# Grouping and order of the row transfers of an RMSNorm-matmul kernel: 40 tiles of input loaded at the outset, the first eight output tiles stored as one transfer, then loads and stores of eight tiles in turn

## The chip, the cores and the metric

The kernel runs on one core of one Trainium2 chip. The core has TensorE (PE, matrix products and transposes, written to PSUM), VectorE (DVE), ScalarE (ACT), GpSimd (POOL) and SyncE (SP), which here only issues transfers. Transfers between HBM and the on-chip memory run on the core's 16 DMA engines. The metric is the device time of one execution in microseconds (us); the number given for a kernel is the median of its timed runs. The times of the kernel before are 209.05, 209.08 and 209.09 us, so the median is 209.08.

## The reference

```python
batch, seq, dim, out_dim = 16, 1024, 512, 768
rms = np.sqrt(np.mean(x ** 2, axis=-1, keepdims=True) + eps)
x_norm = x / rms * gamma
return np.matmul(x_norm, weight).astype(np.float32)
```

`x` is 16384 rows of 512 float32 (33.55 MB), `weight` is 512 x 768 (1.57 MB), the output 16384 rows of 768 float32 (50.33 MB).

## The kernel before

The 16384 rows are cut into 128 *tiles* of 128 rows, one row to a partition. A tile of x is 262,144 bytes (2 KB to a partition), a tile of the output 393,216 bytes (3 KB to a partition). Two tiles make a *pair* `j`, and the main loop runs over the pairs 1 to 63 (pair 0 is written out ahead of it).

A tile passes these stages. SP loads it into `xt`, which has 2 buffers of 16 tiles, that is 32 tile places; tile `i` and tile `i + 32` share a place (`x_of`). POOL casts it to bf16 (`cast`, L187, into `xb`; four tiles of every 16 go by `cast_quad`, L259, into `xq`). ACT sums its squares (`square`, L195); a place of `xt` is free for the next load when both the cast and the squares of its tile are done. PE transposes the bf16 tile as 32-bit words (L229) and DVE copies the result out of PSUM (L238), or, for the tiles of `xq`, DVE transposes blocks (L270). PE multiplies with the weights (`matmuls`, L299). ACT for even tiles (L278) and DVE for odd ones (L280) scale the product by the row's reciprocal root and write it to `ot`, which has 3 buffers of 8 tiles; tile `i` and tile `i + 24` share a place. SP stores a finished group of tiles from there (`store`, L292).

All transfers but the small one of gamma are issued by SP, one after the other, in the order in which the program text makes them: the class `Order` records every operation, puts each on its engine's list in that order, and adds the waits on semaphores that reads and writes of the same cells need. If a transfer on SP has to wait, everything behind it on SP waits too.

What the change touches is the size of the transfers and their order.

- `stretches` (called for `x_first, x_size` and `o_first, o_size`) tells how tiles are grouped into transfers. Before, x is loaded as 2, 2, 4 and 8 tiles, then 8 and 8, then 16 three times (tiles 32 to 79), then 8 each. The output is stored as 1, 1, 2 and 4 tiles, then 8 each, and at the end as 4, 4, 4, 2 and 2.
- `rows` tells which rows of HBM a transfer has. A block of `t` tiles is laid so that each partition holds `t` consecutive rows; a transfer of `n` of them moves, for each partition, one piece of `n` rows. Before, `t` is the size of the load for the first 16 tiles, 16 for the next 16, and 32 from there on. So a load of 16 tiles moves pieces of 32 KB, one of 8 tiles pieces of 16 KB, a store of 8 tiles pieces of 24 KB, and the store of one tile pieces of 3 KB.
- `load_until` issues the loads up to a tile. Ahead of the loop it is called for 32 tiles (with the two weight transfers between the first and the second load). In the loop, the call at the head of a pair's turn decides when SP is given further loads; `AHEAD` is 20.

The order of transfers on SP before is therefore: the loads of tiles 0 to 31; the stores of tiles 0, 1, 2 to 3, 4 to 7; the load of 32 to 47; the stores of 8 to 15 and 16 to 23; the load of 48 to 63; the stores of 24 to 31 and 32 to 39; the load of 64 to 79; and so on, two stores and then 16 tiles of loads; after the last load (112 to 127) come the stores of tiles 88 to 127.

Of the kernel before, what the change touches and what calls it, by code (L numbers as in the profile page):

```python
# [100 lines left out]
def kernel(  # L101
# [20 lines left out]
    NT = N // P  # L122
    NP = NT // 2
    XG, OG = 16, 8
    AHEAD = 20

    def stretches(group, parts):
        first, size, i = {}, {}, 0
        for g in range(NT // group):
            for n in parts.get(g, [group]):  # L130
                for t in range(i, i + n):
                    first[t], size[t] = i, n
                i += n
        return first, size

    last = NT // OG - 1
    x_first, x_size = stretches(XG, {0: [2, 2, 4, 8], **{g: [8, 8] for g in (1, 5, 6, 7)}})
    o_first, o_size = stretches(OG, {0: [1, 1, 2, 4], last - 1: [4, 4], last: [4, 2, 2]})

    def rows(ap, i, n):  # L140
        base, t = (x_first[i], x_size[i]) if i < XG else (i - i % XG, XG) if i < 2 * XG else (i - i % (2 * XG), 2 * XG)
        return ap[base * P:(base + t) * P, :].rearrange("(p t) d -> p t d", t=t)[:, i - base:i - base + n, :]

    def sb(name, shape, dtype):
# [29 lines left out]
    def load(i):  # L174
        dst, to = x_of(i, x_size[i])
        order.transfer(SP, lambda: SP.dma_start(out=dst, in_=rows(x, i, x_size[i])), writes=to)  # L176
# [3 lines left out]
    def load_until(i):  # L180
        while starts and starts[0] < i:
            load(starts.pop(0))

    def cast(i, n=1):
        src, of = x_of(i, n)
        s = i // 8 % 2
        run(POOL, lambda: POOL.tensor_copy(out=xb[s][:, i % 8:i % 8 + n, :], in_=src), of, cells("xb", s, i % 8, n))  # L187
# [17 lines left out]
    def norms(i, n):  # L205
        for t in range(n):
            square(i + t)
        root(i, n)
# [6 lines left out]
    def norms_of_group(j):  # L215
        square(2 * j)
        square(2 * j + 1)
        if j in norm_end:
            root(*norm_end[j])
# [33 lines left out]
    def quad_of(j):  # L253
        return j // 2 if (2 * j) % XG >= XG - 4 and 2 * j >= XG else None

    def cast_quad(q):
        src, of = x_of(4 * q, 4)
        s = 4 * q // XG % 2
        run(POOL, lambda: POOL.tensor_copy(out=xq[s], in_=src), of, [("xq", s)])  # L259
        for t in range(4):  # L260
            xT_of[4 * q + t] = (xTq[s][:, t], ("xTq", s))
        words = xq[s].rearrange("p t d -> p (t d)").bitcast(F32).rearrange("p (a w) -> p a w", w=P)
        turned = xTq[s].rearrange("p t h m c -> p (t h m c)").bitcast(F32).rearrange("p (a m) -> p a m", m=P)
        for tokens in range(0, P, B):
            for features in range(0, P, B):
                quad_moves.append((turned[features:features + B, :, tokens:tokens + B],
                                   words[tokens:tokens + B, :, features:features + B], s))
# [4 lines left out]
    def move_quad(n):  # L272
        for _ in range(min(n, len(quad_moves))):
            move(*quad_moves.pop(0))
# [9 lines left out]
    def accumulator():  # L284
        return next(turns) % 3

    def store(i):
        first, n = o_first[i], o_size[i]
        s = first // OG % 3
        if i == first + n - 1:  # L290
            src = ot[s][:, first % OG:first % OG + n, :]
            order.transfer(SP, lambda: SP.dma_start(out=rows(out, first, n), in_=src), reads=cells("ot", s, first % OG, n))  # L292
# [12 lines left out]
    def matmuls(i, a, ks, feed=None):  # L305
        block, cell = xT_of[i]
        for k in ks:
            lhsT = block[:, k // 2, :, k % 2]
            hold(lhsT, cell)
            for half, lo, hi in ((0, 0, WIDE), (1, WIDE, O)):  # L310
                product(ops[a][:, lo:hi], lhsT, w_bf[:, k, lo:hi], k == 0, k == K - 1,
                        [cell, ("w", k, half)], [("ops", a, half)])
            if feed:
                feed()

    def finish_tile(i, a, engine):
        s = i // OG % 3

        before = [("ot", s, i % OG - 1)] if i == o_first[i] + o_size[i] - 1 else []
        scale(engine, ot[s][:, i % OG, :], ops[a][:, :O], rstd[:, i:i + 1],  # L320
              [("ops", a, 0), ("ops", a, 1), ("rstd", i)] + before, [("ot", s, i % OG)])
        store(i)

    def feeder(pairs, gaps, alone=False):
        queue = [(j, t, h) for j in pairs for t in range(2) for h in range(2)]
        calls = iter(gaps)

        def feed():
            for _ in range(next(calls)):
                j, t, h = queue.pop(0)  # L330
                transpose_word(j, t, h)
                if alone and h == 1:
                    evac(j, t, 1)
                elif (t, h) == (1, 1):
                    evac(j)
        return feed
# [65 lines left out]
    mid, one, two, both = ([0, 0, 1, 1, 0, 1, 1, 0], [1, 1, 0, 1, 1, 0, 0, 0], [1, 0, 1, 0, 1, 0, 1, 0],  # L402
                           [1, 1, 1, 1, 1, 1, 1, 1])
    for j in range(1, NP):
        load_until((2 * j + AHEAD + XG - 1) // XG * XG)
        if j in (1, 2):
            cast(4 * j + 4, 4)
        elif j % 8 == 4 and j + 4 < NP:
            cast(2 * j + 8, 8)
        elif j % 8 == 6 and j + 2 < NP:  # L410
            cast(2 * j + 12, 4)
        if (2 * j + 2) % XG == 0 and 2 * j + 2 < NT:
            cast_quad((2 * j + 2 + XG - 4) // 4)
        elif 2 * j >= XG:
            move_quad(3)
        if j < 4:
            norms(2 * j + 2, 2)
        for pair in norm_turns.get(j, []):
            norms_of_group(pair)
        if j < 3:  # L420
            feed = feeder([j + 1], mid if j == 1 else one, alone=j == 1)
        elif j == 3:
            feed = feeder([4, 5], both)
        elif j + 2 < NP and quad_of(j + 2) is None:
            feed = feeder([j + 2], two)
        else:
            feed = None
        for i, engine in ((2 * j, ACT), (2 * j + 1, DVE)):
            a = accumulator()
            matmuls(i, a, range(K), feed)  # L430
            finish_tile(i, a, engine)
# [48 lines left out]
```

## Time and profile before

| what | value |
|---|---|
| median of the timed runs | 209.08 us |
| the profiled execution: its time, its span | 208.56 us, 206.8 us |
| instructions in the span | 2761 |
| ACT busy, DVE busy, POOL busy | 144.5, 149.3, 59.9 us |
| HBM read, written | 35.13 MB, 50.33 MB |
| TensorE clock granted, mean | 0.992 |
| loads of 2048 KB, issue to landing | median 21.0 us (9 of them) |
| loads of 4096 KB, issue to landing | median 22.7 us (3) |
| stores of 3072 KB, issue to landing | median 16.5 us (13) |

The span is the stretch that the profile shows; the execution's time holds 1.8 us more around it. Busy times are sums over the span. "Issue to landing" is the time from SP's issuing instruction to the semaphore that tells that all of a transfer has landed; it holds the time that the transfer spends behind earlier ones. A transfer's issue is short (0.33 us for a store): SP is free again long before the data has moved.

### The profile page before, as it was taken

Reading aid. Unit: us, or ns where it says so; the run is one execution under the profiler, and the core shown is the slowest. Engines: PE = TensorE matmul, PEld = TensorE weight load, DVE = VectorE, ACT = ScalarE, POOL = GpSimd, SP = SyncE. Lnnn points to the kernel's source line nnn. Section 1 sums busy time; section 2 is a strip of 40 time slices with the busy share of each in tenths; the row PEclk is TensorE's granted clock in tenths of the full one; section 3 lists DMA queues with packets and bytes.
Section 4 is the critical chain, followed back from the end, with each engine's and each line's share of the span. In section 5 each row is a group of like instructions: output and inputs, shape, how many; then the busy total and the mean of one; then the engine's idle time right before and its main releaser. Section 6 shows DMA issues by size and latency. Waiting matters only on the chain.

```text
span 206.8 us, 2761 instructions
## 1 busy us (share of the span) xinstructions
PE 192.9 (93%) x1212; PEld 72.5 (35%) x717; DVE 149.3 (72%) x255; ACT 144.5 (70%) x343; POOL 59.9 (29%) x34
## 2 busy tenths in 40 slices
PE   7789999999999999998999999999999999999930
PEld 1234443432343333342333333433343333343300
DVE  0455647998589966998469984999569984999520
ACT  4798897868768496864977687677867787673310
POOL 2247651009300291004900660006700274000000
PEclk9999999999999999999999999999999999999996
DMA  6999999999999999999999999999999999999993
GB/s 225 423 445 428 387 385 444 456 396 428 428 445 425 417 426 455 425 409 433 431 415 436 428 445 403 439 417 447 418 441 414 437 433 441 418 442 409 414 415 141
DMA packets 5632, 85.62 MB, mean 414 GB/s; under 512 B 626, under 2 KB 628, under 8 KB 1780
## 3 DMA queue, kind: packets, MB, share of 16 engines
q1 hardware_dynamic: 5616, 85.46, 97.6%
q8 instruction: 7, 0.11, 0.2%
q14 instruction: 5, 0.04, 0.0%
q10 hardware_dynamic: 4, 0.00, 0.0%
HBM read 35.13 MB, written 50.33 MB: 413 GB/s over the span
## 4 chain that ended last, share of the span: by engine, by line
PE 71%; DMA 16%; DVE 5%; issue 2%; SPq 1%; ACT 1%; POOL 1%; ACTq 0%
PE ps L299 62%; DMA xt<-in_x_dram 16%; PE ps L229 8%; DVE ot L280 2%; DVE xTq L270 2%; DVE xT L238 1%; POOL xb L187 1%; ACT jk L195 0%; SPq L344 0%; SPq L176 0%; ACT ot L278 0%; SPq L292 0%; DVE rstd L202 0%; SPq L475 0%; ACTq L93 0%
## 5 line engine op out<-in xcount | busy, mean ns | idle before, releaser
L299 PE MATMUL ps<-w_bf,xT 128*128 128x256 bf16 (+1 forms) x783 | 144.9, 325 | 2.6 <-DVE w_bf L280 0.8
L278 ACT ACTIVATE ot<-ps,rstd 128x768 f32<-128x768 f32 x64 | 57.4, 897 | 42.3 <-PE ps L299 40.7
L195 ACT ACTIVATE jk<-xt 128x512 bf16<-128x512 f32 x128 | 78.8, 619 | 7.7 <-DMA xt<-in_x_dram 7.7
L187 POOL CAST xb<-xt 128x2048 bf16<-128x2048 f32 (+3 forms) x21 | 46.3, 2221 | 111.9 <-DMA xt<-in_x_dram 93.3
L280 DVE TENSOR_SCALAR ot<-ps,rstd 128x768 f32<-128x768 f32 x64 | 64.8, 1013 | 9.4 <-PE ps L299 8.7
L295 PEld LDWEIGHTS <-xT 128*128 128x128 bf16 x400 | 39.3, 98 | 60.2 <-issue 52.1
L229 PE MATMUL ps<-ident_f,xb 128*128 128x128 f32 x200 | 54.1, 274 | 0.9 <-POOL xb L187 0.9
L238 DVE COPY xT<-ps 128x1024 bf16<-128x1024 bf16 (+1 forms) x53 | 34.5, 653 | 24.0 <-PE ps L229 22.3
L270 DVE STREAM_TRANSPOSE xTq<-xq 32x256 f32<-32x256 f32 x112 | 48.7, 435 | 3.4
L229 PEld LDWEIGHTS ps<-ident_f,xb 128*128 128x128 f32 x200 | 28.2, 142 | 46.5 <-issue 42.7
L299 PE MATMUL ps<-w_bf,xTq 128*128 128x256 bf16 (+1 forms) x217 | 41.8, 324 | 0.4
L195 ACT ACTIVATION_READ_ACCUMULATOR jk<-xt 128x1 f32 x128 | 24.3, 190 | 0.0
L295 PEld LDWEIGHTS <-xTq 128*128 128x128 bf16 x112 | 11.0, 98 | 14.5 <-issue 14.5
L259 POOL CAST xq<-xt 128x2048 bf16<-128x2048 f32 x7 | 13.3, 1897 | 0.0
L202 DVE RECIPROCAL rstd<-rms 128x8 f32<-128x8 f32 (+3 forms) x20 | 3.9, 193 | 8.3 <-ACT rms L200 8.1
L200 ACT ACTIVATE rms<-ssq,eps_sb 128x8 f32<-128x8 f32 (+3 forms) x20 | 6.0, 300 | 0.7
L299 PE MATMUL ps<-warm 128*128 128x512 bf16 x10 | 4.4, 578 | 1.4 <-DVE eps_sb L353 1.4
L278 ACT ACTIVATE w_bf<-w_f,g_sb 128x768 bf16<-128x768 f32 x2 | 1.9, 936 | 1.1 <-DMA w_f<-in_weight_dram 1.1
L376 DVE COPY g_sb<-ps 128x4 f32<-128x4 f32 x1 | 0.2, 163 | 3.2 <-PE ps L370 3.2
L340 ACT ACT_TABLE_LOAD x1 | 1.3, 1283 | 1.5 <-SPq L434 1.5
L280 DVE TENSOR_SCALAR w_bf<-w_f,g_sb 128x512 bf16<-128x512 f32 (+2 forms) x3 | 1.4, 481 | 0.6 <-DMA w_f<-in_weight_dram 0.6
L370 PEld LDWEIGHTS ps<-ident_f,g_row 2*128 2x128 f32 x2 | 0.3, 202 | 2.6 <-issue 2.6
(10 smaller groups left out, 1.9 us busy)
## 6 DMA issues: line engine op xcount, KB each, us to landing
out_dram<-ot SPq DMA_DIRECT2D x13, 3072.0 KB, 16.5
xt<-in_x_dram SPq DMA_DIRECT2D x9, 2048.0 KB, 21.0
xt<-in_x_dram SPq DMA_DIRECT2D x3, 4096.0 KB, 22.7
out_dram<-ot SPq DMA_DIRECT2D x4, 1536.0 KB, 11.5
out_dram<-ot SPq DMA_DIRECT2D x3, 768.0 KB, 7.3
w_f<-in_weight_dram SPq DMA_DIRECT2D x2, 768.0 KB, 5.5
xt<-in_x_dram SPq DMA_DIRECT2D x2, 512.0 KB, 5.2
xt<-in_x_dram SPq DMA_DIRECT2D x1, 1024.0 KB, 9.0
```

The lines of the kernel that those rows point to most:

```text
L187: run(POOL, lambda: POOL.tensor_copy(out=xb[s][:, i % 8:i % 8 + n, :], in_=src), of, cells("xb", s, i % 8, n))
L195: run(ACT, lambda: ACT.activation(out=jk[j], in_=src[:, 0, :], func=AF.Square, accum_out=ssq[:, i:i + 1]), of, [("jk", j), ("ssq", i)])
L200: run(ACT, lambda: ACT.activation(out=rms[:, s], in_=ssq[:, s], func=AF.Sqrt, scale=1.0 / D, bias=eps_sb), [("ssq", t) for t in range(i, i ...
L202: run(DVE, lambda: DVE.reciprocal(out=rstd[:, s], in_=rms[:, s]), [("rms", i)], [("rstd", t) for t in range(i, i + n)])
L229: run(PE, lambda: PE.transpose(out=tp[b][:, t, h, :], in_=words[:, lo:lo + P], identity=ident_f), cells("xb", s, j % 4 * 2 + t) + ["ident" ...
L238: run(DVE, lambda: DVE.tensor_copy(out=dst[:, t:t + n, :], in_=src[:, t:t + n, :]), [("tp", b)], cells("xT", j % 4, t, n))
L259: run(POOL, lambda: POOL.tensor_copy(out=xq[s], in_=src), of, [("xq", s)])
L270: run(DVE, lambda: DVE.transpose(out=dst, in_=src), [("xq", s)], [("xTq", s)])
L278: run(ACT, lambda: ACT.mul(out=dst, in_=src, mul=r), reads, writes)
L280: run(DVE, lambda: DVE.tensor_single_scalar(out=dst, in_=src, scalar=r, op=mybir.AluOpType.mult), reads, writes)
L295: run(PE, lambda: PE.ldweights(lhsT), [cell])
L299: run(PE, lambda: PE.add_instruction(mybir.InstMatmult(name=nc.get_next_instruction_name(), engine=mybir.EngineType.PE, ins=[PE.lower_ap(r ...
```

## The change

Three things are changed, all of them in what SP issues.

- Loads are of 8 tiles from tile 8 on (no loads of 16), the first eight tiles still as 2, 2 and 4. Tiles 0 to 7 of the output are stored as one transfer of 3 MB; the end of the output is as before.
- The layout in `rows` follows: `t` is 8 for the first 16 tiles, in the input and the output, then 16, then 32. So the loads of tiles 0 to 1 and 2 to 3 have pieces of 4 KB that lie 16 KB apart in HBM, and the load of 4 to 7 has pieces of 8 KB that lie 16 KB apart. They were gapless before.
- `AHEAD` is 40 and the call in the loop rounds down to 8 tiles. At pair 1 it asks for tiles 32 to 39, at pair 4 for 40 to 47, and from there at every fourth pair for eight more.

The order of transfers on SP becomes: the loads of tiles 0 to 31 as 2, 2, 4, 8, 8, 8; the load of 32 to 39, which waits for POOL and ACT (the places of tiles 0 to 7); the store of 0 to 7; the load of 40 to 47, which waits for ACT; the store of 8 to 15; the load of 48 to 55; and so on in turn up to the load of 120 to 127, which follows the store of 80 to 87; then the stores of 88 to 127 as before. Both kernels issue 39 transfers on SP: 15 loads of x, 2 of weights and 22 stores before, 18, 2 and 19 after. The lists of the other engines keep their instructions and their order.

```diff
-    AHEAD = 20
+    AHEAD = 40
...
-    x_first, x_size = stretches(XG, {0: [2, 2, 4, 8], **{g: [8, 8] for g in (1, 5, 6, 7)}})
-    o_first, o_size = stretches(OG, {0: [1, 1, 2, 4], last - 1: [4, 4], last: [4, 2, 2]})
+    x_first, x_size = stretches(OG, {0: [2, 2, 4]})
+    o_first, o_size = stretches(OG, {last - 1: [4, 4], last: [4, 2, 2]})
 
     def rows(ap, i, n):
-        base, t = (x_first[i], x_size[i]) if i < XG else (i - i % XG, XG) if i < 2 * XG else (i - i % (2 * XG), 2 * XG)
+        t = OG if i < XG else XG if i < 2 * XG else 2 * XG
+        base = i - i % t
         return ap[base * P:(base + t) * P, :].rearrange("(p t) d -> p t d", t=t)[:, i - base:i - base + n, :]
...
-        load_until((2 * j + AHEAD + XG - 1) // XG * XG)
+        load_until((2 * j + AHEAD) // OG * OG)
```

## The prediction

> **What bounds the kernel now.** I read the page's queue rows first, then the windows table (busy time by engine, granted clock, share of the 16 DMA engines, GB/s), then single transfers from issue to landing.
>
> ```profile
> PE 192.9 (93%) x1212; PEld 72.5 (35%) x717; DVE 149.3 (72%) x255; ACT 144.5 (70%) x343; POOL 59.9 (29%) x34
> ...
> q1 hardware_dynamic: 5616, 85.46, 97.6%
> ```
>
> Two resources are nearly full: PE with 192.9 us of a span of 206.8, and SP's queue q1, whose packets took 97.6% of the 16 engines' span, 201.8 us. The windows tell which of them sets the end:
>
> ```profile
> 22.00:27.00 5.00, 4.95 (x34) 2.04 (x20) 3.32 (x5) 4.30 (x14) 3.32 (x1) 1.00 0.97 343
> 27.00:31.00 4.00, 3.95 (x27) 1.61 (x16) 1.93 (x4) 3.97 (x11) 2.73 (x2) 1.00 1.04 428
> 41.00:49.00 8.00, 7.95 (x52) 2.92 (x29) 7.64 (x14) 5.92 (x13) 2.78 (x1) 1.00 1.01 424
> 64.00:72.00 8.00, 7.95 (x53) 2.91 (x29) 7.61 (x15) 4.47 (x12) 0.75 (x1) 1.00 0.97 412
> 88.00:96.00 8.00, 7.95 (x53) 2.96 (x30) 7.60 (x15) 3.48 (x8) 0.31 (x1) 1.00 0.97 412
> 112.00:120.00 8.00, 7.95 (x53) 2.93 (x30) 7.64 (x14) 5.77 (x14) 3.60 (x1) 1.00 1.03 434
> 136.00:144.00 8.00, 7.95 (x52) 2.90 (x29) 7.61 (x15) 5.98 (x14) 3.60 (x1) 1.00 1.02 432
> 160.00:168.00 8.00, 7.95 (x53) 2.78 (x29) 7.60 (x15) 6.30 (x15) 3.60 (x1) 1.00 1.05 448
> 5.00:200.00 195.00, 189.31 (x1204) 71.97 (x713) 148.90 (x252) 142.52 (x341) 58.52 (x27) 1.00 1.01 426
> 200.00:202.00 2.00, 0.00 (x0) 0.00 (x0) 0.00 (x0) 0.00 (x0) 0.00 (x0) 1.00 1.00 415
> 202.00:204.00 2.00, 0.00 (x0) 0.00 (x0) 0.00 (x0) 0.00 (x0) 0.00 (x0) 0.83 0.58 240
> ```
>
> From 5 to 200 us the DMA share is 1.01 at 426 GB/s, and it is still 1.00 at 200 to 202 us, when PE has stopped; then some DMA engines run dry before others (0.58). The two last stores, of 768 KB each, tell the same:
>
> ```profile
> 196.65 0.33 SPq L292 DMA_DIRECT2D out_dram<-ot  x1
> out_dram<-ot SPq DMA_DIRECT2D x1, 768.0 KB, 7.3
> ...
> 199.52 0.33 SPq L292 DMA_DIRECT2D out_dram<-ot  x1
> out_dram<-ot SPq DMA_DIRECT2D x1, 768.0 KB, 6.3
> ```
>
> They land at 203.95 and 205.82, 1.87 us apart; 0.786 MB at 426 GB/s is 1.85 us. So the last store went directly behind the one before it, although it was issued 2.87 us later. What would it take alone? The first load (512 KB) lands 3.4 us after its issue with an empty queue; 0.262 MB more is 0.6 us, so 4.0 us. It took 6.3: the queue was 2.3 us behind PE. The end is set by one continuous stretch of transfers, and PE could be up to 2.3 us later, or any amount earlier, without moving it. Any gain or loss must come from the queue: its bytes, its rate, or a gap.
>
> **Bytes.** 33.55 MB of x, 1.57 of weights and 50.33 of output in both, and 39 transfers in both: zero. Pieces of 16 KB in place of 32 KB for tiles 32 to 79: zero too, since 5 to 200 us holds both kinds and the late windows with 16 KB loads (434, 432, 448) are not below those with 32 KB loads (424, 412, 412).
>
> **Gaps.** The queue runs dry only if SP holds a transfer back too long. The outset, 9.96 MB, ends at 2.0 + 9.96/0.426 = 25.4 us (first packets at about 2.0 us: 0 to 5 us has a share of 0.59). New is the wait of the load of 32 to 39 for the casts and squares of tiles 0 to 7. Queued behind it are the store of 0 to 7 and all the rest of SP.
>
> ```profile
> 18.88 0.19 ACT L195 ACTIVATION_READ_ACCUMULATOR jk<-xt 128x1 f32 x1
> 19.10 0.29 ACT L200 ACTIVATE rms<-ssq,eps_sb 128x2 f32<-128x2 f32 x1
> ```
>
> The last squares of tile 7 end at 19.07 us, 6.3 us before the queue is empty, and the store behind it cannot go before tile 7 is scaled (23.76 us, when the store of 4 to 7 is issued now). So the wait costs nothing; without that cover it would cost what it exceeds 25.4 us by. From here each eight tiles put 5.24 MB into the queue, 12.3 us, while PE takes 11.7 us for them (the stores of 8 to 15 and 24 to 31 are issued at 35.58 and 59.00, 23.42 us for two groups). The queue ends at 30.3 with 32 to 39, 37.7 with the store, 42.6 with 40 to 47 (its squares are done by 25.78, when the load of 32 to 47 is issued now), and the next store comes at 35.6. The backlog is 7 us there and grows: no gap.
>
> **The stores come later: what is late next.** A load sits ahead of each store, so a place of `ot` comes free later; tile i+24 waits for the store of tile i. Tightest is where the backlog is largest.
>
> ```profile
> out_dram<-ot SPq DMA_DIRECT2D x1, 3072.0 KB, 22.7
> 165.68 0.90 ACT L278 ACTIVATE ot<-ps,rstd 128x768 f32<-128x768 f32 x1 [0.24 <-PE ps L299]
> ...
> 177.17 0.90 ACT L278 ACTIVATE ot<-ps,rstd 128x768 f32<-128x768 f32 x1 [0.92 <-PE ps L299]
> ```
>
> The store of 88 to 95, issued at 153.55, lands now at 176.25, 0.9 us ahead of tile 112's scaling (177.17). In the changed order everything from the load of 120 to 127 on has the same bytes ahead of it: unchanged. The store of 80 to 87 goes behind the load of 112 to 119, one 4.9 us load later than now: it lands one such load ahead of 120 to 127 (168.9), at 164.0, and tile 104's scaling is at 165.68: 1.7 us spare. Earlier stores have more. Cost zero; a miss would be paid only beyond the 2.3 us that PE is ahead.
>
> **PE.** Now PE loses 0.7 us at 95 to 98, when the 4 MB load of 64 to 79 lands late (95.57). In the new order those tiles land as two loads, the first well ahead. PE gains 0.7 us, ACT's waits for loads go: worth nothing, by the 2.3 us.
>
> **Rate: the one place where something moves.** Two terms, both at changes of direction, where stores follow loads in the queue.
>
> First, at 22 to 27 us, the end of the outset loads and the first small stores, 343 GB/s against 426: 5 x (1 - 343/426) = 0.97 us lost. The change puts more loads there and one store of 24 KB pieces behind them. Bounds: all of it comes back (-1.0), or it moves to 30 us with the change of direction (0). The small stores themselves, 27 to 31 us, run at 428, which speaks against their size as the cause; the later changes, with large stores, lose far less, which speaks for it. I take half, -0.5.
>
> Second, there are 7 such changes of direction now (after the outset and after six blocks of loads) and 12 in the new order: 5 more. The price of one from the six later windows: at most (1 - 412/426) x 8 = 0.26 us, at least 0 (three windows are above the mean). Between, 0.13: +0.65; bounds 0 and +1.3.
>
> Sum: -0.5 + 0.65 = +0.15 us on 208.56, so 208.71 for such an execution. The median of the runs shown lies 0.52 above the profiled one, so 209.08 + 0.15 = 209.2.
>
> **Two rules of the Trainium skill.** The page "DMA: Bandwidth & Descriptors", in "Anatomy of one DMA", gives a transfer about 2.0 us of fixed cost; four stores in one would save 3 x 2.0 = 6 us if these costs added up, making 203. The two stores above, landing 1.87 us apart, show no fixed cost in a full queue; I don't use it. The same page, "Latency and other measured facts", speaks against the new layout: a large power-of-two pitch between the partitions' rows slowed copies, to 207 GB/s at 512 KiB. The nearest row here, 16 KB pieces 32 KB apart (tiles 16 to 23, inside 5 to 22 us), runs at 430 GB/s. By the page's figure the first 8 tiles' 2.1 MB would take 5.3 us more, as an estimate: 214; no run here shows pieces 16 KB apart.
>
> **Rivals.** *The dip goes and direction costs nothing* (0.22): for it, 434, 432 and 448 at the changes with 16 KB loads, which is what all are now; against, the dip lies in reads of 16 KB pieces. 208.1, up to 208.6 with a little direction cost. *Direction costs* (0.30): the dip stays and each of five more changes costs 0.26 us: 210.4; it is slower from 0.42 us on, that is from 0.09 apiece with the dip kept. For it 412 twice; against, the later windows. *The output buffers decide* (0.05): stores land late against `ot`, PE stops at tiles 104 or 112; to show at the end it has to be over 1.7 (0.9) + 2.3 us late: 210 to 212. That the change isn't done as written is ruled out by SP's list of instructions, which has the new order.
>
> **How the numbers follow.** No change by over 0.2% (0.42 us, about what a measurement can tell) 0.43; the first rival makes faster 0.22; the other two make slower 0.35. The range goes from all of the dip gained (208.1) to all of the direction cost (210.4); the forecast's own is 208.7 to 209.5.
>
> **What would show it.** DMA share 1.0 from 5 to 200 us; first change of direction near 30 us, its dip there or gone; ACT and DVE without waits for stores; the last two stores again 1.9 us apart. I am wrong if the share drops in mid-span, if the last store lands 4 us after its issue (then PE sets the end), or if the loads before 11 us run well below 430 GB/s.

## The result, and the profile after

| | median, us | runs |
|---|---|---|
| before | 209.09 | 6 |
| changed | 242.71 (241.72 to 244.18) | 6 |

The ratio is 1.1617, with a 95% interval of 1.1592 to 1.1643: the change makes the kernel 16% slower, 33.6 us. The forecast was 209.2 with a range of 208.1 to 210.4. The profiled execution took 241.72 us, with a span of 239.8 us. Ratios and intervals count undisturbed executions alone; of those reported below, one of run e6 was disturbed (it took 419.45 us).

One thing has to be known to read its time rightly. The changed kernel scales tiles 4 to 7 by the squares of tiles 36 to 39, and tiles 12 to 15 by those of 44 to 47, so what it writes for these eight tiles is not what the reference asks for. In the text of the loop the load stands above the squares:

```python
    for j in range(1, NP):
        load_until((2 * j + AHEAD) // OG * OG)
...
        if j < 4:
            norms(2 * j + 2, 2)
        for pair in norm_turns.get(j, []):
            norms_of_group(pair)
```

At pair 1 the load of tiles 32 to 39 is recorded first; then `norms(4, 2)` reads the place of tile 4, whose last writer is now that load. The same happens at pair 4 with the load of 40 to 47 and the squares of 12 to 15. From pair 8 on the squares of a place stand ahead of its next load again.

Before, PE is busy for 70% or more of every slice but the last two (the page cuts the span into 40 equal slices; a digit is the busy share in tenths), and ACT waits for loads only briefly (the row gives us in total, times, longest):

```profile
PE   7789999999999999998999999999999999999930
ACT jk L195 <- DMA xt<-in_x_dram: 7.7, 6, 3.0
```

These are rows of the page of the changed kernel: busy time, the slices of 6.0 us for PE, the granted clock and the DMA share, and the main queue.

```profile
PE 197.5 (82%) x1212; PEld 73.6 (31%) x717; DVE 149.1 (62%) x255; ACT 144.4 (60%) x343; POOL 60.0 (25%) x34
PE   6970019900699999999999999999999999999990
PEclk9997558975599999999999999999999999999999
DMA  6999920497008999999999999999999999979787
q1 hardware_dynamic: 5616, 85.46, 85.3%
```

Bytes and packets are what they were (85.46 MB, 5616 packets), and so are the counts of instructions that compute (PE 1212, DVE 255, ACT 343, POOL 34). But PE has two holes, and the queue runs dry towards the end of each of them: its packets took 97.6% of the span before, 85.3% now. The holes lie in the first 62 us; from there on PE is full to its end.

The answer on waits of the changed kernel (engine, line, what it waited for; us in total, times, longest) names them. Three of its lines, the long waits of ACT and PE in the holes:

```profile
ACT jk L196 <- DMA xt<-in_x_dram: 39.5, 4, 19.6
PE ps L300 <- DVE xT L239: 18.3, 1, 18.3
PE ps L300 <- ACT ot L279: 14.2, 1, 14.2
```

And the timelines of ACT, SP and PE around the holes (start, duration, instruction, idle time before it and its releaser):

```profile
12.33 0.88 ACT L279 ACTIVATE ot<-ps,rstd 128x768 f32<-128x768 f32 x1
32.80 0.63 ACT L196 ACTIVATE jk<-xt 128x512 bf16<-128x512 f32 x1 [19.59 <-DMA xt<-in_x_dram]
```

```profile
15.32 0.33 SPq L177 DMA_DIRECT2D xt<-in_x_dram  x1
```

```profile
16.22 0.49 PE L300 MATMUL ps<-w_bf,xT 128*128 128x512 bf16 x2
35.04 0.82 PE L300 MATMUL ps<-w_bf,xT 128*128 128x512 bf16 x2 [18.33 <-DVE xT L239]
```

ACT scales tile 0 at 12.33 us. Its next instruction is the square of "tile 4", and that is held until the load of 32 to 39 has landed: issued at 15.32, it stands behind the whole outset in the queue and lands at 32.8. The scaling of tile 2 stands behind that square on ACT, and DVE stands behind ACT (its reciprocal waits 20.2 us for ACT's root). DVE's next copy of transposed tiles out of PSUM stands behind that reciprocal, PE waits for the copy, and stops for 18.3 us. No tile is finished meanwhile, so no store is issued, and at about 31 us the queue is empty as well (the last three figures of a row are the granted clock, the DMA share and GB/s):

```profile
30.00:35.00 5.00, 0.00 (x0) 0.00 (x0) 0.50 (x3) 2.16 (x6) 0.00 (x0) 0.50 0.27 115
35.00:40.00 5.00, 4.96 (x24) 1.90 (x15) 2.53 (x5) 3.73 (x11) 1.38 (x1) 0.73 0.00 0
```

The second hole is the same again:

```profile
41.63 0.88 ACT L279 ACTIVATE ot<-ps,rstd 128x768 f32<-128x768 f32 x1
59.26 0.63 ACT L196 ACTIVATE jk<-xt 128x512 bf16<-128x512 f32 x1 [16.75 <-DMA xt<-in_x_dram]
```

```profile
44.68 0.35 SPq L293 DMA_DIRECT2D out_dram<-ot  x1
45.08 0.43 SPq L177 DMA_DIRECT2D xt<-in_x_dram  x1
72.44 0.34 SPq L293 DMA_DIRECT2D out_dram<-ot  x1
```

The load of 40 to 47 is queued on SP behind the store of 0 to 7. That store can go only when tile 7 is scaled, at 44.68; the load goes 0.4 us later and lands after 14.2 us; until then ACT waits for it with the square of "tile 12", and PE waits for ACT. The next store goes only at 72.44, and the queue is empty from about 58 us until then.

The sum closes on the last instructions. DVE's last scaling starts at 198.20 before and at 234.19 after: 36.0 us later. The last store, issued at 199.52 before, landed 6.3 us later; after, it is issued at 235.49 and lands 3.4 us later, because the queue is no longer behind: -2.9. That makes 33.1; the spans differ by 33.0. Of the 36.0 us, 32.5 are the two stops. The other 3.5 fit three small terms, as an estimate: PE starts 1.3 us later (first product with the weights at 8.58 in place of 7.28 us); in the windows of its two restarts the granted clock is 0.73 (35 to 40 us, PE busy 4.96) and 0.50 (60 to 65 us, PE busy 3.24), which is 4.96 x 0.27 + 3.24 x 0.50 = 3.0 us of work not done; and the stop of 0.7 us that PE had before is gone.

### The profile page after: what moved, and what is told of

The parts are those of the page before. It is cut to its first block, busy times and chain, and to the rows that moved or that the text cites. A ratio compares the mean times of both kernels' runs of the same rounds, so it can differ in the third digit from the quotient of the medians.

```text
span 239.8 us, 2758 instructions
## 1 busy us (share of the span) xinstructions
PE 197.5 (82%) x1212; PEld 73.6 (31%) x717; DVE 149.1 (62%) x255; ACT 144.4 (60%) x343; POOL 60.0 (25%) x34
## 3 DMA queue, kind: packets, MB, share of 16 engines
q1 hardware_dynamic: 5616, 85.46, 85.3%
## 4 chain that ended last, share of the span: by engine, by line
PE 75%; DMA 18%; ACT 2%; DVE 1%; SPq 1%; issue 1%; POOL 1%
PE ps L300 66%; DMA xt<-in_x_dram 18%; PE ps L230 8%; ACT jk L196 1%; POOL xb L188 1%; DVE ot L281 1%; DVE xT L239 0%; SPq L177 0%; ACT ot L279 0%; SPq L345 0%; SPq L293 0%; ACT rms L201 0%; DVE rstd L203 0%; SPq L476 0%; SPq L435 0%
## 5 line engine op out<-in xcount | busy, mean ns | idle before, releaser
L300 PE MATMUL ps<-w_bf,xT 128*128 128x256 bf16 (+1 forms) x783 | 148.5, 330 | 33.7 <-DVE xT L239 18.3
L230 PE MATMUL ps<-ident_f,xb 128*128 128x128 f32 x200 | 55.0, 279 | 1.2 <-POOL xb L188 1.2
```

The costliest lines, as they stand in the source:

```text
L230: run(PE, lambda: PE.transpose(out=tp[b][:, t, h, :], in_=words[:, lo:lo + P], identity=ident_f), cells("xb", s, j % 4 * 2 + t) + ["ident" ...
L300: run(PE, lambda: PE.add_instruction(mybir.InstMatmult(name=nc.get_next_instruction_name(), engine=mybir.EngineType.PE, ins=[PE.lower_ap(r ...
```

## The experiments

Two theories. **A**: the order of the operations. The squares of 4 to 7 and 12 to 15 stand behind the loads that overwrite their places, so ACT, and PE behind it, waits for those loads. **B**: the transfers themselves. The order of loads and stores on SP, or the slower first loads, makes data late whatever the squares do. The first four runs tell them apart, and the last of the eight checks A's size. The others ask what the rest of the change is worth.

**e1: the loads behind the squares.** Transfers, their order on SP and their layout are those of the changed kernel.

```diff
-    AHEAD = 40
+    AHEAD = 34
```

> AHEAD 34 in place of 40: the load of tiles 32 to 39 is made at pair 3, behind the squares of tiles 4 to 7, and that of 40 to 47 at pair 7, behind the squares of 12 to 15. The order of transfers on SP stays that of the changed kernel, so do sizes and layout. Theory A (the squares of 4 to 7 and 12 to 15 stand behind the load that overwrites their places, so ACT waits for that load and PE stops behind ACT for 18.3 and 14.2 us): both stops go, 242.7 - 32.5 = 210.2, between 209 and 211.5. Theory B (the order of loads and stores on SP, or the slower first loads with 16 KB pitch, makes the transfers late): same order and layout, so still near 242.

Measured: 209.12 us beside 208.98 before, ratio 0.9999 (0.9986 to 1.0013). Both stops are gone, and the changed order of transfers is worth nothing against the kernel before. What ACT waits for loads in it:

```profile
ACT jk L196 <- DMA xt<-in_x_dram: 3.1, 2, 2.8
```

B falls here: nothing on SP was moved but the time from which a load is allowed (17.22 us for the load of 32 to 39, 15.32 in the changed kernel). That this time is not the cause either is shown by e4.

**e2 and e3: one of the two early loads alone.**

```diff
-        load_until((2 * j + AHEAD) // OG * OG)
+        load_until((2 * j + (34 if j < 4 else 40)) // OG * OG)   # e2: second early
+        load_until((2 * j + (40 if j < 3 else 34)) // OG * OG)   # e3: first early
```

> As e1 but the load of tiles 40 to 47 stays at pair 4, ahead of the squares of tiles 12 to 15 (these then sum the squares of tiles 44 to 47, so that these four tiles are scaled by other rows' roots). Theory A: ACT reaches the square of tile 12 near 26 us and waits for the load of 40 to 47, which has the outset, the load of 32 to 39 and the store of 0 to 7 ahead of it in the queue and lands near 45 us; some 2 us are covered by PE's accumulators: one stop of about 17 us, 227 (224 to 230), and no stop before 20 us. Theory B: near 242.

Measured: 229.80 us (one run), inside the range. The waits of PE and ACT in it:

```profile
ACT jk L196 <- DMA xt<-in_x_dram: 27.2, 3, 24.0
PE ps L300 <- ACT ot L279: 21.3, 1, 21.3
```

> As e1 but the load of tiles 32 to 39 stays at pair 1, ahead of the squares of tiles 4 to 7 (these then sum the squares of tiles 36 to 39). Theory A: the first stop alone, 18 us of PE from 17 us on, 210.2 + 18.3 = 228.5 (226 to 231). Theory B: near 242.

Measured: 227.21 us (one run), inside the range.

```profile
ACT jk L196 <- DMA xt<-in_x_dram: 22.5, 3, 19.3
PE ps L300 <- DVE xT L239: 18.0, 1, 18.0
```

Each early load makes its own stop, and the stop its own loss: 21.3 us of PE and 20.8 us of time for e2, 18.0 and 18.2 for e3. Together they are less than the sum, 33.6 in place of 39.0. In e2 the load of 40 to 47 is issued at 25.58 us into a full queue and ACT waits 24 us for it; in the changed kernel the first stop has emptied the queue, and the load has only one store ahead of it.

**e4: the squares ahead, the loads where they are.** This undoes the order from the other side.

```diff
+        if j == 1:
+            norms(4, 2)
+            norms(6, 2)
+        if j == 4:
+            norms_of_group(6)
+            norms_of_group(7)
         load_until((2 * j + AHEAD) // OG * OG)
```

(The later calls for these squares are taken out.)

> The loads stay where the changed kernel makes them (pairs 1 and 4), and the squares of tiles 4 to 7 and of 12 to 15 are put ahead of them on ACT instead. SP's order and the layout are those of the changed kernel. Theory A: no stop, 209 to 212 (the squares come up to two pairs earlier on ACT and may delay a scaling by 1 to 2 us at the start). Theory B: near 242.

Measured: 209.22 us, ratio 1.0016 (1.0000 to 1.0033); ACT's longest wait for a load is 2.9 us. An early load as such costs next to nothing; what cost 33 us was the work that stood behind it.

**e8: the load one pair later.**

```diff
-    AHEAD = 40
+    AHEAD = 36
```

> The changed kernel with AHEAD 36: the load of tiles 32 to 39 is made at pair 2, behind the squares of tiles 4 and 5 and ahead of those of 6 and 7 (which then sum the squares of tiles 38 and 39); that of 40 to 47 is made at pair 6, behind all squares that it has to follow. Theory A: one stop, which begins one pair (3.0 us of PE) later than in e3 and ends with the same landing near 32 us: 227.2 - 3.0 = 224 (222 to 226). If it is the number of tiles that are scaled by a late load that counts: half of e3's loss of 18, 218.

Measured: 224.61 us (one run). The load lands at the same time (ACT goes on at 32.85 us, 32.80 in the changed kernel), and PE stops later, for 15.5 us in place of 18.0 in e3:

```profile
ACT jk L196 <- DMA xt<-in_x_dram: 20.1, 3, 16.8
PE ps L300 <- DVE xT L239: 15.5, 1, 15.5
```

So the loss runs from the place of the misplaced square in ACT's order to the landing of the load: with two tiles concerned in place of four the stop is 2.5 us shorter, near the one pair by which it begins later, and not half as long.

**e5, e6, e7: the first eight tiles.** In e1 the first load lands 4.6 us after its issue, 3.4 before; and the dip of 22 to 27 us (343 GB/s before) is not there. These three ask whether one can have the fast start and no dip.

e5 is e1 with the first eight tiles as before:

```diff
-        t = OG if i < XG else XG if i < 2 * XG else 2 * XG
-        base = i - i % t
+        t = x_size[i] if i < XG else XG if i < 2 * XG else 2 * XG
+        base = x_first[i] if i < XG else i - i % t
...
-    o_first, o_size = stretches(OG, {last - 1: [4, 4], last: [4, 2, 2]})
+    o_first, o_size = stretches(OG, {0: [1, 1, 2, 4], last - 1: [4, 4], last: [4, 2, 2]})
```

> As e1 (loads behind the squares, eights from tile 8 on), but the first eight tiles as in the kernel before: gapless loads of 2, 2 and 4 and stores of 1, 1, 2 and 4. The first load lands at 3.4 us after issue in place of 4.6. If the dip of 22 to 27 us came from the small stores queued behind the outset loads, it is back here (near 343 GB/s) and the time is that of before and e1, 209.1 within 0.4. If it came from something else that e1 took away (the load of 16 tiles behind), the dip stays away and the 0.8 to 1.2 us of the first loads are gained: 208.0 to 208.4.

Measured: 209.47 us, ratio 1.0036 (1.0022 to 1.0050). The first load lands after 3.3 us, and the dip is back (351 GB/s).

e6 is e1 with the eight tiles laid out as four gapless pairs and stored as one transfer:

```diff
-    x_first, x_size = stretches(OG, {0: [2, 2, 4]})
+    x_first, x_size = stretches(OG, {0: [2, 2, 2, 2]})
...
-        t = OG if i < XG else XG if i < 2 * XG else 2 * XG
+        t = 2 if i < OG else OG if i < XG else XG if i < 2 * XG else 2 * XG
...
+        if n > t:
+            return ap[i * P:(i + n) * P, :].rearrange("(b p t) d -> p b (t d)", p=P, t=t)
```

> As e1, but the first eight tiles are laid out as four gapless blocks of two tiles: loads of 2, 2, 2 and 2 with no gaps, still one store of 3 MB for tiles 0 to 7, now in pieces of 6 KB. If the pitch of 16 KB made the first loads slow, the first load lands 3.4 us after issue again; if the dip belongs to small stores of separate transfers, it stays away: 209.1 - 1.0 = 208.1 (207.8 to 208.6). If small pieces bring the dip, 209.1.

Measured: 209.82 us (the median of five executions), ratio 1.0039 (1.0024 to 1.0053), slower than both values expected. The first load lands after 3.3 us, 22 to 27 us runs at 429 GB/s, and the dip comes later, with the one store: 346 GB/s at 27 to 31 and 370 at 31 to 35 us.

e7 is the kernel before with the layout of 8 rows to a partition for the first 16 tiles, in the loads and in the stores (`rows` serves both):

```diff
-        base, t = (x_first[i], x_size[i]) if i < XG else
+        base, t = (i - i % OG, OG) if i < XG else
```

> The kernel before with one thing changed: the layout of the first 16 tiles has 8 rows to a partition, so that the first loads have pieces of 4 and 8 KB that lie 16 KB apart (and the stores of 1, 1, 2 and 4 tiles pieces that lie 24 KB apart). If the pitch costs what the first loads show, the first load lands 4.6 us after its issue in place of 3.4 and the time is 209.1 + 0.6 to 1.2 = 209.7 to 210.3. If the slow first loads have another cause: 209.1.

Measured: 209.35 us, ratio 1.0028 (1.0015 to 1.0040), a loss of 0.6 us by the ratio; the time is below the 209.7 to 210.3 us expected of a costly pitch. The first load lands after 4.7 us. The dip leaves 22 to 27 us (416 GB/s), and another shows at 41 to 49 (374, 424 before).

The windows table puts the five side by side. Before:

```profile
0.00:12.00 12.00, 9.03 (x39) 2.56 (x23) 3.49 (x13) 7.37 (x15) 3.06 (x10) 1.00 0.86 347
12.00:50.00 38.00, 37.42 (x242) 14.68 (x147) 27.39 (x47) 31.87 (x82) 16.75 (x9) 1.00 1.01 418
```

e1:

```profile
22.00:27.00 5.00, 5.00 (x36) 2.09 (x21) 2.94 (x6) 4.31 (x11) 3.60 (x1) 1.00 1.01 429
0.00:12.00 12.00, 9.25 (x32) 2.17 (x18) 2.54 (x9) 6.08 (x12) 2.92 (x9) 1.00 0.83 313
12.00:50.00 38.00, 37.56 (x245) 14.83 (x148) 27.05 (x48) 31.96 (x82) 19.23 (x10) 1.00 1.01 430
```

e5, then e6, then e7:

```profile
12.00:50.00 38.00, 37.56 (x245) 14.78 (x147) 27.41 (x48) 31.88 (x82) 19.72 (x10) 1.00 1.01 413
```

```profile
12.00:50.00 38.00, 37.47 (x246) 14.80 (x147) 27.21 (x48) 31.71 (x82) 18.70 (x9) 1.00 1.01 416
```

```profile
12.00:50.00 38.00, 37.89 (x249) 15.05 (x149) 27.13 (x48) 31.98 (x83) 15.82 (x8) 1.00 1.01 413
```

e1 loses 12 x (347 - 313)/426 = 1.0 us in the first 12 us and gains 38 x (430 - 418)/426 = 1.1 us up to 50 us, which fits that it equals the kernel before. These rows are from single executions (e7's took 209.97 us, the slowest of its ten; e1's 209.13 beside 208.56 before), so terms of about 1 us are argued from them and not shown. Neither e5 nor e6 kept both the start and the gain. e5's return of the dip fits small stores as its cause, e6's dip with one store in small pieces fits small pieces, but in e7 the stores are small and the dip is elsewhere. Its cause stays open; no version was found that beats the kernel before.

## Why the prediction was wrong

**The step that failed** is this one, under "Gaps": "New is the wait of the load of 32 to 39 for the casts and squares of tiles 0 to 7", covered because "the last squares of tile 7 end at 19.07 us, 6.3 us before the queue is empty". That the place of a tile is free after its cast and its squares is true of the kernel's intent; which squares the load waits for is decided by the order in which operations are recorded. At pair 1 only the squares of tiles 0 to 3 are recorded. The load waited for those and for the casts, and went at 15.32 us, earlier than forecast; the squares of 4 to 7 then waited for the load, to 32.8 us. The forecast looked for what stands behind the load on SP, and not for who reads the places that the load writes. It called the wait free; what stands in its place, the wait of the squares for the load, stops PE for 18.0 us in e3, and for the load of 40 to 47 ("its squares are done by 25.78") for 21.3 us in e2.

The evidence was in the program text. The instructions and the order on the other engines were unchanged, as the forecast's document said; but what ACT's squares of tiles 4 and 12 wait for had become the new loads. So the statement there that the load of 32 to 39 waits for ACT on the places of tiles 0 to 7 holds for the squares of tiles 0 to 3 alone.

**The end is set by the queue, PE has 2.3 us to spare: right for the order meant, wrong for the change.** With the stops, PE set the end: the last store landed 3.4 us after its issue, within the 4 us named as the sign for this.

```profile
out_dram<-ot SPq DMA_DIRECT2D x1, 768.0 KB, 3.4
```

Even this store was not alone: the last two land 1.86 us apart again, at 237.03 and 238.89, and the DMA share is 0.94 or more from 231 to 238 us. So a store alone takes at most 3.4 and not the estimated 4.0 us, and the queue was at least 2.9 us behind PE before. In e1 the last two stores take 7.4 and 6.3 us, as before, and the DMA share is 1.00 from 5 to 200 us.

**Bytes: zero: right. The layout: missed.** The forecast gave the first loads' 16 KB pitch no price of its own. The first load lands 1.2 us later in the changed kernel and e1 (4.6 against 3.4), and e7 shows a loss of 0.6 us for the layout alone (of loads and stores together). The Trainium skill's page "DMA: Bandwidth & Descriptors", section "Latency and other measured facts", had the sign right, for copies at pitches of 512 KiB and more, which no run here has; its figure would have made the loss 5.3 us, as the forecast's estimate, and the measurement decides. The 2.0 us of fixed cost that the forecast quoted and did not use stand in that page's section "Anatomy of one DMA" for transfers issued by GpSimd; all large ones here are issued by SP.

**The dip: half of 1.0 us, 1.1 us** gained between 12 and 50 us in e1's trace. **Direction: 0.65 us, not seen in the sum.** e1 has the 12 changes of direction; its windows around some later ones read 408 (49 to 57 us), 418 (72 to 80), 423 and 419 GB/s, so some cost may be there, but its rate from 5 to 200 us is 427 against 426, and 209.12 holds all terms together, by these windows a gain of 1.1 at the dip and a loss of 1.0 in the first loads. For the order that was meant, the forecast's +0.15 us was near the zero that e1 measured, and in part by luck: a term that it left out (the first loads) about made up for one that it had too small (the dip).

**The output buffers: right.** Neither the changed kernel nor e1 shows a wait of ACT or DVE for a store.

**The rivals.** None of the four named this mechanism; the chance of 0.35 given to slower was given for direction and buffers, which were not it. The one that asked whether the change does what it says looked only at SP's list.

## What to carry to other kernels

When a load is made earlier into a reused place, list every reader of the old contents and see that each is recorded ahead of the load; a planner that derives waits from program order will otherwise give the reader a wait for the new data. Compare what each instruction waits for in the two programs, not only the order of the instructions. Here a stall of ACT, with the scalings behind it on ACT's list, cost the time from the misplaced instruction's turn to the landing of the late transfer, and as no finished tile left meanwhile, a full queue drained and its cover was lost too.

## What was not expected of the hardware

The first loads react to how their pieces lie in HBM: a load of 4 KB pieces 16 KB apart lands 4.6 to 4.7 us after its issue, one of gapless pieces after 3.3 to 3.4. PE's granted clock is 0.56 in the first full 5-us window of the first stop (20 to 25 us), 0.50 in the next two, and 0.73 in the 5 us after it, so a stop puts PE back by a little more than its length. And the loss of rate at the first change from loads to stores, 343 GB/s over 5 us, moved when the layout of the first tiles' loads and stores was changed (e7); which of the two did it is not shown.
